# A hybrid decoder block on one core: new durations in the kernel's own scheduler, and one probability tile for two heads

## The chip, the cores and the metric

The kernel runs on one core of one Trainium2 chip. The metric is the device time of one execution in microseconds. The kernel does all its arithmetic in fp32: each large matrix product is made of three products of split operands (a high part times a high part, and two cross products of a high and a low part).

## The reference, cut to what matters

One decoder layer over 512 tokens of width 1024, then a final RMSNorm. The layer has one input projection whose columns feed three groups of heads, an output projection, and a feed-forward block of width 4096:

```
h = rmsnorm(x, norm1_w)
proj = h @ w_in
aq, ak, av, bq, bk, bv, br, ba, cq, ck, cv = split(proj)
y_a = dilated_attention(aq, ak, av, bias_a)          # 6 heads of 64
y_b = gla(bq, bk, bv, br, ba, w_a2, b_a, gla_norm_w)  # 4 heads, gated linear attention
y_c = moba_attention(cq, ck, cv, bias_c)              # 6 heads of 64
x = x + concat(y_a, y_b, y_c) @ w_out
x = x + square(relu(rmsnorm(x, norm2_w) @ w_ff1)) @ w_ff2
return rmsnorm(x, final_norm_w)
```

With 512 tokens the two kinds of softmax attention are plain causal attention with a bias that depends on the distance alone (a table of 640 values for each head), so the kernel treats the 12 heads of groups A and C alike, as six pairs.

## The kernel before, in words

**Stages.** The kernel first multiplies x with the columns for the gated linear attention (products `av`, `bq`, `bk`, until about 29 us), then makes queries and keys of the twelve softmax heads (`qkps`, two pieces of weights for each pair of heads, q and k), values and gates (`vps`), the gated linear attention (`lp`, `ktp`, `up`, `op`, `yp`), and for each pair of heads scores (`sps`), softmax, transposes (`ptp`) and values (`po`). Then come the output projection (`ops`), the norm and transposes (`yps`), and the feed-forward block in four slices of two layers (`f1X`, `f1Y`, `f1Z`, then `f2X`, `f2Y`, `f2Z`). The four large projections use a scheme of seven block products in place of eight, whose sums of weight blocks are made partly by accumulating DMA loads from POOL's queue.

**Weights.** Every piece of 128x1024 weights (`wraw`, 512 KB) is loaded, then cut: ScalarE rounds it to the high part `wh`, VectorE subtracts to make the low part `wl` (function `parts`). Activations are cut in the same way (`xh`/`xl`, `xsh`/`xsl`, `Ah`/`Al`).

**The start.** `scaled_x` makes `xh`, `xl` and the squares of x. `row_scale` sums the squares on TensorE (`rsp`) after six of the eight passes of the first product, and makes on VectorE `ss`, with ScalarE and VectorE `rstd`, then `diag` and the scale row `R`. `load_small` (L622) copies one column of x on POOL (tile `xT2`), so that what follows waits for that piece of x, and then issues ten loads of constants on POOL's queue: `cst`, `smask`, `hsel`, the bias table's inputs, `bav`, `wa2`, two pieces of `oneh`, `lmask` and `gw`.

**What sets the order.** No order is written out by hand. Each part of the work is a generator ("stream") that yields operations, waits for events, and takes and gives back counted resources (PSUM banks, weight buffers). The class `Plan` is a list scheduler that runs when the kernel is built: it keeps a clock for each engine, a time at which each tile is ready, and a clock each for the descriptor generator (`dge`) and for DMA. Among the operations at the heads of all streams it issues the one that can start first by its clocks, with the stream's priority to break ties. Issue order is queue order on the engine, so a wrong duration in the planner makes another order, not another duration. The durations stand in `Op.__init__` (`self.cost`, in microseconds):

- TensorE: an fp32 product with a contraction over 32 rows (the `lp` products of the gated linear attention, 112 of them) costs 0.031.
- VectorE: 0.075 + 1.04 ns an element, half the rate for copies and operations with scalars whose inputs are all in SBUF. There is no price of its own for the scan, for the masked copies (`copy_predicated`, which put the levels of the gated linear attention into `attn`), or for an operand that is one column read per partition.
- DMA: an ordinary load takes 0.47 on the `dge` clock, and its bytes at 320e3 per microsecond on the `dma` clock, whichever engine issues it, and is there 2.0 later.

Where an operation can run on either of two engines (`Any`), the planner takes the one that ends first. That is so for the scaling of probabilities by `rz` (VectorE or ScalarE) and for the copies of `th`, `q` and `k`.

Slots: most tiles of 128x512 or less share one tag of 52 buffers (`slot`). The planner does not count them; an operation that writes a slot still in use waits on the chip without the planner knowing. In `attention`, each head takes three slots for its probabilities: `P0` for query block 3, `P1` for blocks 2 and 0, and `P2`, half used, for block 1. `softmax` works on these in place: minimum and sum (`tensor_tensor_reduce`, written as `mn`), exponential on ScalarE with the sum `z`, reciprocal `rz`, and the scaling.

Of the kernel before, what the change touches and what calls it, by code (L numbers as in the profile page):

```python
# [9 lines left out]
F32 = mybir.dt.float32  # L10
# [26 lines left out]
class Op:  # L37


    def __init__(self, eng, method, args, kw):  # L40
        self.eng, self.method, self.args, self.kw = eng, method, args, kw
        self.out = args[0]
        outs = [args[0]]
        inner = [a for a in list(args[1:]) + [v for k, v in kw.items() if k != "accum_out"] if isinstance(a, bass.AP)]
        if kw.get("accum_out") is not None:
            outs.append(kw["accum_out"])
        if method == "tensor_tensor_reduce":
            outs.append(inner.pop())
        self.outs = [o.tensor.name for o in outs]
        self.ins = [a.tensor.name for a in inner] + (self.outs if "accum_op" in kw else [])  # L50
        n = 1
        for c in args[0].shape[1:]:
            n *= c
        self.mode = None
        if eng == "tensor":
            self.mode = inner[-1].shape[0] in (32, 64), args[0].shape[0] in (32, 64)
            wide, long = inner[-1].dtype == F32, max(n, 250) / 2400
            if method != "matmul":
                self.cost = 0.109
            elif wide and inner[-1].shape[0] == 32:  # L60
                self.cost = 0.031
            elif wide:
                self.cost = 0.002 + max(n / 600 / (1 + (args[0].shape[0] == 64)), 0.21)
            elif inner[-1].shape[0] == 64:
                self.cost = max(n / 2260, 0.12) / 2
            else:
                self.cost = 0.0135 + long
        elif eng == "scalar":
            few = sum(a.shape[-1] == 1 and n > 4 for a in inner) + ("accum_out" in kw)
            self.cost = 0.09 + n / 1200 + 0.093 * few  # L70
        elif eng == "vector":
            many = method in ("tensor_scalar", "tensor_copy") and all(a.space == bass.MemoryType.SB for a in inner)
            rate = 0.52 if many else 6.25 if method == "reciprocal" else 1.04
            if method == "tensor_reduce":
                n = 512
            self.cost = 0.075 + n * rate / 1000
        elif eng == "gpsimd":
            self.cost = 0.15 + n * (0.9 if method == "memset" else 2.1) / 1000
        if method == "dma_start":
            self.cost = 0.9 if "accum_op" in kw else 0.06  # L80
            self.rate = 170e3 if "accum_op" in kw else 320e3
            self.size = 4 * n * args[0].shape[0]
# [18 lines left out]
PE, ACT, DVE, POOL, SP = (Engine(n) for n in ("tensor", "scalar", "vector", "gpsimd", "sync"))  # L101


class Plan:
# [18 lines left out]
    def fire(self, key, t=None):  # L123
        self.done[key] = self.now if t is None else t
# [7 lines left out]
    def issue(self, op, at):  # L132
        getattr(getattr(self.nc, op.eng), op.method)(*op.args, **op.kw)  # L133
        t = self.start(op, at)
        end = t + op.cost
        if op.mode:
            end += SWITCH * (self.mode not in (None, op.mode))
            self.mode = op.mode
        self.clock[op.eng] = end
        if op.method == "dma_start":  # L140
            if "accum_op" in op.kw:
                self.clock["dma"] = max(self.clock["dma"], end + 1.0) + op.size / op.rate
                end = self.clock["dma"] + 3.0
            else:
                self.clock["dge"] = max(self.clock["dge"], t) + 0.47
                self.clock["dma"] = max(self.clock["dma"], self.clock["dge"] + 0.65) + op.size / op.rate
                end = self.clock["dma"] + 2.0
        for n in op.outs:
            self.ready[n] = max(self.ready.get(n, 0.0), end + self.LAT)
        return end  # L150
# [59 lines left out]
def hybrid_block_kernel(ctx: ExitStack, tc: tile.TileContext, xT_d, x_d, w0_d, wv_d, wqk_d, wo_d, w1_d, w2_d,  # L210
                        nw_d, ba_d, wa2_d, gw_d, fw_d, rb_d, oh_d, cst_d, lm_d, out_d):
    nc = tc.nc
    consts = ctx.enter_context(tc.tile_pool(name="consts", bufs=1))
# [10 lines left out]
    def slot(name, dt=F32, shape=(128, 512)):  # L224
        return sp.tile(list(shape), dt, name=name, tag="slot", bufs=SLOTS)
# [37 lines left out]
    alT = slot("alT", shape=(128, 512))  # L263
    xT = [slot("xT") for _ in range(KT)]
    tab = dr.tile([12, 640], F32, name="tab")
    xT2 = consts.tile([128, 1], F32)
    R, Rn8, ssx = slot("R"), slot("Rn8"), slot("ssx")
    xh = [slot("xh", F32R) for _ in range(KT)]
    xl = [slot("xl", F32R) for _ in range(KT)]
# [351 lines left out]

    def load_small():  # L622
        yield ("wait", ("xh", 1))
        yield POOL.tensor_copy(xT2, xT[2][:, :1])
        for t, d in ((cst, cst_d[:, 0:512]), (smask, cst_d[:, 512:1024]), (hsel, cst_d[:, 1024:1028]), (rb[:34, :12], rb_d),
                     (bav, ba_d), (wa2[:16], wa2_d)):
            yield POOL.dma_start(t, d)
        for i in range(2):
            yield POOL.dma_start(oneh[i][:34], oh_d[:, i * 320:(i + 1) * 320])
        fire("consts")  # L630
        spawn(bias_table(oneh), 1)
        yield POOL.dma_start(lmask, lm_d)
        yield POOL.dma_start(gw, bass.AP(tensor=gw_d.tensor, offset=gw_d.offset, ap=[[0, 128], [1, 256]]))
# [317 lines left out]
    def attention():  # L951

        yield ("wait", "tab")
        yield ("wait", "attn")
        for p in range(6):
            nb = []
            for e in range(2):
                nb.append(slot("nb"))
                yield SP.dma_start(nb[e], bass.AP(tensor=tab.tensor, offset=tab.offset + (2 * p + e) * 640, ap=[[1, 128], [1, 512]]))
            yield ("wait", ("qk", p))  # L960
            (qh, ql), (kh, kl) = st[p]
            P = []
            for e in range(2):
                A0, A1, A2 = slot("P0"), slot("P1"), slot("P2", shape=(128, 256))
                P.append([A1[:, 384:512], A2[:, 0:256], A1[:, 0:384], A0[:, 0:512]])
            for qbs in ((3, ), (2, 0, 1)) if p in (1, 2, 3, 4) else ((3,), (2, 0), (1,)):
                apart = len(qbs) > 1 and 1 in qbs
                sps, sps1 = [], []
                for e in range(2):
                    yield ("take", "s")  # L970
                    sps.append(bank("s", "sps"))
                    if apart:
                        yield ("take", "og"[e])
                        sps1.append(bank("og"[e], "sps"))
                ops, at, n0 = [], {}, 0
                for qb in qbs:
                    n = 128 * (qb + 1)
                    qs = slice(qb * 128, (qb + 1) * 128)
                    for e in range(2):
                        at[qb, e] = sps1[e][:, :n] if apart and qb == 1 else sps[e][:, n0:n0 + n]  # L980
                    for j, (qq, kk) in enumerate(((qh, kh), (ql, kh), (qh, kl))):
                        for e in range(2):
                            rows = slice(64 * e, 64 * e + 64)
                            ops.append(PE.matmul(at[qb, e], qq[rows, qs], kk[rows, :n], start=(j == 0), stop=(j == 2),
                                                 skip_group_check=True))
                    if not (apart and qb == 1):
                        n0 += n
                yield ops
                last = [x for x in qbs if not (apart and x == 1)][-1]
                for qb in qbs:  # L990
                    for e in range(2):
                        free = "og"[e] if apart and qb == 1 else "s" if qb == last else None
                        spawn(softmax(P[e][qb], at[qb, e], nb[e][:, 384 - 128 * qb:512], (p, e, qb), free), 1)
            give("big")
            give("big")
            if p == 5:
                give("w")
                fire("scores")
            for kbs in KBS:
                for e in range(2):  # L1000
                    spawn(turn(P[e], kbs, (p, e)), 0)

    turns = []

    def turn(P, kbs, key):
        for qb in range(min(kbs), NB):
# [6 lines left out]
        for kb in kbs:  # L1013
            off[kb] = n
            for qb in range(kb, NB):
                ops.append(PE.transpose(pt[:, n:n + 128], P[qb][:, kb * 128:(kb + 1) * 128], flip))
                n += 128
# [36 lines left out]

    def softmax(P, s, nb, key, last):
        mn, z, rz = (small(x, (128, 1)) for x in ("mn", "z", "rz"))
# [716 lines left out]
```

## Time and profile before

| | us |
|---|---|
| three runs | 564.97, 565.54, 566.04 |
| median | 565.54 |
| the profiled execution's own time | 565.34 |
| its span in the profile | 563.5 |

The span runs from the first to the last instruction that the profiler recorded; what lies around it is 1.84 us. The granted TensorE clock was 0.998 of full speed over the execution. In the rows that follow, a name such as `wl<-wraw,wh` says which tile an instruction writes and which it reads, `x138` how many such instructions there are, and a name after `<-` in an idle time says what ended it. PE is TensorE, PEld its weight loads, DVE VectorE, ACT ScalarE, POOL GpSimd and SP SyncE. All instructions carry the line of the planner's `issue` (L133), so groups are told apart by tile names.

### The profile page before, as it was taken

To read this page: it belongs to the slowest core of one execution; us is meant where nothing else is said; L and a number is where in the kernel's file an instruction comes from. 1 tells how busy PE (TensorE), PEld (TensorE's weight loads), DVE (VectorE), ACT (ScalarE), POOL (GpSimd) and SP (SyncE) were. 2 spreads that over 40 slices of the span, in tenths; PEclk is the share of its full clock that TensorE was granted. 3 is DMA by queue.
4 is the path that set the end of the run, shared out by engine and by line. 5 is a ranking of instruction groups with operands and counts; after the bars stand their busy time and mean duration, and the time that the engine had idled before them with its cause. 6 is when DMAs were issued, how large, how long until landed. Compare 5 with 4: busy or idle time off the path is not lost.

```text
span 563.5 us, 9460 instructions
## 1 busy us (share of the span) xinstructions
PE 554.7 (98%) x3513; PEld 478.4 (85%) x3513; DVE 480.4 (85%) x875; ACT 370.7 (66%) x658; POOL 69.7 (12%) x91
## 2 busy tenths in 40 slices
PE   9999999999999999999999999999999999999995
PEld 8978887867876768899987899988999888999884
DVE  7799999977868988999699995799957799867985
ACT  8664655884865775989766476855477654579553
POOL 5031110010000002110111010120020110011203
PEclk9999999999999999999999999999999999999999
DMA  8954685585124775992989429687378594395803
GB/s 317 393 123 123 128 217 124 161 335 103 38 43 127 242 150 115 271 272 60 274 212 204 163 64 278 201 151 204 113 158 283 121 201 158 95 220 113 150 12 137
DMA packets 29948, 96.58 MB, mean 171 GB/s; under 512 B 3648, under 2 KB 3690, under 8 KB 29904
## 3 DMA queue, kind: packets, MB, share of 16 engines
q0 software_dynamic: 9456, 33.53, 32.8%
q1 hardware_dynamic: 20160, 62.20, 31.5%
q8 instruction: 27, 0.44, 0.3%
q10 hardware_dynamic: 288, 0.27, 0.1%
q14 instruction: 17, 0.14, 0.1%
HBM read 93.86 MB, written 2.13 MB: 170 GB/s over the span
## 4 chain that ended last, share of the span: by engine, by line
PE 83%; DVE 11%; ACT 2%; issue 2%; DMA 2%; ACTq 0%; POOLq 0%
PE f2X L133 14%; PE f1X L133 13%; PE qkps L133 11%; PE f1Z L133 8%; PE ops L133 7%; PE f2Z L133 7%; PE f1Y L133 4%; PE vps L133 3%; PE f2Y L133 3%; DVE wl L133 3%; PE po L133 2%; PE ptp L133 2%; PE sps L133 2%; PE av L133 2%; DMA wraw<-in_w 2%
## 5 line engine op out<-in xcount | busy, mean ns | idle before, releaser
L133 DVE TENSOR_TENSOR wl<-wraw,wh 128x1024 fp32r<-128x1024 f32 (+2 forms) x174 | 192.0, 1111 | 38.2 <-ACT wh L133 37.2
L133 ACT ACTIVATE wh<-wraw 128x1024 fp32r<-128x1024 f32 (+2 forms) x173 | 164.7, 966 | 58.9 <-DMA wraw<-in_w 10.5
L133 PE MATMUL f1X<-yp,wh 128*128 128x256 f32 x512 | 92.7, 283 | 0.0
L133 PEld LDWEIGHTS f1X<-yp,wh 128*128 128x128 f32 x512 | 80.1, 192 | 0.3
L133 POOL DMA_DIRECT2D wraw<-in_w x46 | 40.8, 962 | 270.3 <-DVE wl L133 219.0
L133 PE MATMUL f1X<-yp,wl 128*128 128x256 f32 x256 | 72.5, 283 | 0.0
L133 PE MATMUL f2X<-wh,Al 128*128 128x512 f32 (+1 forms) x132 | 50.5, 383 | 0.0
L133 PE MATMUL f2X<-wh,Ah 128*128 128x512 f32 (+1 forms) x132 | 50.5, 383 | 0.0
L133 PE MATMUL f2X<-wl,Ah 128*128 128x512 f32 (+1 forms) x132 | 50.5, 383 | 0.0
L133 PEld LDWEIGHTS f1X<-yp,wl 128*128 128x128 f32 x256 | 49.1, 192 | 0.2 <-DVE wl L133 0.2
L133 PE MATMUL f1Z<-yp,wh 128*128 128x256 f32 x256 | 46.3, 283 | 0.0
L133 ACT ACTIVATE h<-h 128x512 f32<-128x512 f32 x56 | 34.7, 625 | 10.3 <-DVE h L133 9.8
L133 PE MATMUL qkps<-xh,wh 128*128 128x512 f32 x96 | 40.1, 417 | 0.0
L133 PEld LDWEIGHTS f1Z<-yp,wh 128*128 128x128 f32 x256 | 39.9, 192 | 0.0
L133 ACT ACTIVATE Ah<-h 128x512 fp32r<-128x512 f32 x40 | 24.0, 620 | 21.5 <-DVE h L133 21.5
L133 PE MATMUL qkps<-xh,wl 128*128 128x512 f32 x96 | 37.5, 391 | 0.0
L133 PE MATMUL qkps<-xl,wh 128*128 128x512 f32 x96 | 37.5, 390 | 0.0
L133 ACT ACTIVATE P<-P,mn 128x512 f32<-128x512 f32 (+3 forms) x48 | 26.6, 555 | 16.6 <-DVE mn L133 16.5
L133 PE MATMUL f1Z<-yp,wl 128*128 128x256 f32 x128 | 36.2, 283 | 0.0
L133 DVE TENSOR_TENSOR Al<-h,Ah 128x512 fp32r<-128x512 f32 x40 | 26.9, 687 | 3.2 <-ACT Ah L133 3.1
L133 PEld LDWEIGHTS f2X<-wl,Ah 128*128 128x128 f32 x132 | 24.8, 188 | 4.9
L133 PEld LDWEIGHTS f2X<-wh,Ah 128*128 128x128 f32 x132 | 24.8, 188 | 4.8
(266 smaller groups left out, 1223.9 us busy)
## 6 DMA issues: line engine op xcount, KB each, us to landing
wraw<-in_w SPq DMA_DIRECT2D x66, 512.0 KB, 5.2
wraw<-in_w POOLq DMA_DIRECT2D x46, 512.0 KB, 6.7
wraw<-in_wqk SPq DMA_DIRECT2D x12, 512.0 KB, 6.1
wraw<-in_wv SPq DMA_DIRECT2D x10, 512.0 KB, 8.6
wraw<-in_wv POOLq DMA_DIRECT2D x8, 512.0 KB, 6.0
wraw<-in_wo SPq DMA_DIRECT2D x8, 512.0 KB, 7.2
wraw<-in_wo POOLq DMA_DIRECT2D x8, 512.0 KB, 5.9
nb<-tab SPq DMA_DIRECT2D x12, 256.0 KB, 4.3
```

Of the source, the lines that this page charges most:

```text
L133: getattr(getattr(self.nc, op.eng), op.method)(*op.args, **op.kw)
```

## The change

The planner's prices are edited in five places, the two heads of a pair share the tile of block 1, and a tile is renamed:

- an fp32 product over 32 rows costs 0.0635 instead of 0.031;
- a scan costs 1.13; a masked copy 0.58 if the last dimension of its output is 1, else 0.33;
- any other VectorE operation with a one-column operand (and more than 4 elements), and every `scalar_tensor_tensor`, costs 0.055 more;
- an ordinary load from POOL's queue no longer advances the `dge` and `dma` clocks; it is there 3.0 plus its bytes at 80e3 per microsecond after its issue;
- `P2` becomes one tile of 128x2x256 for both heads, allocated once for each pair;
- the column that `load_small` copies is called `x2c`.

```diff
             elif wide and inner[-1].shape[0] == 32:
-                self.cost = 0.031
+                self.cost = 0.0635
...
             self.cost = 0.075 + n * rate / 1000
+            if method == "tensor_tensor_scan":
+                self.cost = 1.13
+            elif method == "copy_predicated":
+                self.cost = 0.58 if args[0].shape[-1] == 1 else 0.33
+            elif any(a.shape[-1] == 1 and n > 4 for a in inner) or method == "scalar_tensor_tensor":
+                self.cost += 0.055
...
             if "accum_op" in op.kw:
                 self.clock["dma"] = max(self.clock["dma"], end + 1.0) + op.size / op.rate
                 end = self.clock["dma"] + 3.0
+            elif op.eng == "gpsimd":
+                end += 3.0 + op.size / 80e3
             else:
                 self.clock["dge"] = max(self.clock["dge"], t) + 0.47
...
-    xT2 = consts.tile([128, 1], F32)
+    x2c = consts.tile([128, 1], F32)
...
-        yield POOL.tensor_copy(xT2, xT[2][:, :1])
+        yield POOL.tensor_copy(x2c, xT[2][:, :1])
...
             P = []
+            A2 = slot("P2", shape=(128, 2, 256))
             for e in range(2):
-                A0, A1, A2 = slot("P0"), slot("P1"), slot("P2", shape=(128, 256))
-                P.append([A1[:, 384:512], A2[:, 0:256], A1[:, 0:384], A0[:, 0:512]])
+                A0, A1 = slot("P0"), slot("P1")
+                P.append([A1[:, 384:512], A2[:, e], A1[:, 0:384], A0[:, 0:512]])
```

## The prediction, made before the changed kernel was run

> **What bounds the kernel now.** I read the page first, for the spread of work over the engines, then busy time by stage, then the waits of the weight loads, and last the order on VectorE and ScalarE where the stages looked thin.
>
> ```profile
> span 563.5 us, 9460 instructions
> PE 554.7 (98%) x3513; PEld 478.4 (85%) x3513; DVE 480.4 (85%) x875; ACT 370.7 (66%) x658; POOL 69.7 (12%) x91
> PE 83%; DVE 11%; ACT 2%; issue 2%; DMA 2%; ACTq 0%; POOLq 0%
> ```
>
> TensorE is busy 554.7 of 563.5 us and carries 83% of the chain that ended last. No product is added or removed by the change, so only the time in which TensorE does nothing can move. The table by stage says where that is (columns: busy us and count for each engine, granted clock, DMA share, GB/s).
>
> ```profile
> 0.00:24.00 24.00, 22.94 (x141) 21.21 (x141) 16.75 (x32) 17.40 (x30) 7.85 (x20) 1.00 0.95 346
> 24.00:47.00 23.00, 22.86 (x108) 18.00 (x108) 22.45 (x43) 13.50 (x20) 4.29 (x7) 1.00 0.66 190
> 76.00:92.00 16.00, 15.84 (x114) 12.48 (x111) 15.43 (x26) 9.69 (x13) 1.75 (x2) 1.00 0.69 162
> 92.00:106.00 14.00, 13.82 (x87) 11.22 (x85) 14.00 (x47) 7.10 (x18) 0.00 (x0) 1.00 0.32 84
> 106.00:122.00 16.00, 15.81 (x98) 12.04 (x100) 14.48 (x50) 15.52 (x38) 0.00 (x0) 1.00 1.00 366
> 264.00:300.00 36.00, 35.55 (x228) 32.16 (x228) 30.92 (x44) 25.81 (x42) 6.24 (x8) 1.00 0.94 228
> 300.00:555.00 255.00, 255.00 (x1605) 231.97 (x1604) 215.91 (x264) 158.77 (x219) 31.21 (x35) 1.00 0.64 160
> ```
>
> From 300 to 555 us there is nothing to win: 255.00 of 255 busy. Idle TensorE inside these stages is 0.14 + 0.16 + 0.18 + 0.19 + 0.45 = 1.12 us. That is too little, because a matmul's recorded length overlaps the next one's:
>
> ```profile
> 40.28 14.32 PE qkps L133 x63
> ```
>
> ```profile
> 38.63 0.39 PE L133 MATMUL qkps<-xh,wl 128*128 128x512 f32 x1
> 39.15 1.12 PE L133 MATMUL zps<-alT,misc 128*128 128x512 f32 x2
> ```
>
> In the chain 63 projection products take 14.32 us, 227 ns each, while the timeline records one as 0.39 us long; a pause shorter than the difference stays hidden.
>
> The waits of the weight loads between 28 and 125 us show those pauses (in total, times, longest):
>
> ```profile
> PEld sps L133 <- DVE mn L133: 1.0, 3, 0.4
> PEld ptp L133 <- ACT th L133: 0.6, 2, 0.4
> PEld zps L133 <- DVE alT L133: 0.6, 1, 0.6
> PEld ptp L133 <- ACT P L133: 0.6, 1, 0.6
> PEld vps L133 <- DVE v L133: 0.4, 1, 0.4
> PEld lp L133 <- DVE kq L133: 0.4, 1, 0.4
> PEld ptp L133 <- ACT v L133: 0.3, 1, 0.3
> ```
>
> These are 3.9 us, nearly all behind VectorE or behind ScalarE work that follows VectorE. In the same stages VectorE is full: 22.45 of 23 us, 15.43 of 16, 14.00 of 14. So from 24 to 122 us VectorE decides what little TensorE loses, and 3.9 + 0.45 (the stage 264 to 300) = 4.4 us is about the most that a better order could give, outside the head and the tail.
>
> **The change part by part.**
>
> *POOL's plain loads in the planner.* Before, each of load_small's ten loads (L622) adds 0.47 to the planner's descriptor clock and its bytes at 320e3 a microsecond to its DMA clock, ahead of SyncE's later loads. The queue's row for the first 24 us gives the bytes:
>
> ```profile
> q0 software_dynamic: 464, 0.98, 11.3%
> ```
>
> 0.98 MB put about 3.1 on the DMA clock, ten loads 4.7 on the other. After, they touch neither. I followed the two clocks and the three "raw" tokens by hand with the code's constants: the first wqk load lands at plan time 23 before and at about 19.5 after, the second at 25 before and 21 after. The row sums ss, which wait for the product rsp, stand near plan time 23.5 in both, since TensorE's first six passes set them. So before, the order is ss, then the low part wl of the first wqk piece; that is the order on the chip:
>
> ```profile
> 19.33 1.27 DVE L133 SCALAR_TENSOR_TENSOR xs<-xT,nw,xs 128x256 f32<-128x256 f32 x3
> 24.17 0.16 DVE L133 TENSOR_SCALAR ss<-rsp 128x4 f32<-128x4 f32 x1 [3.57 <-PE rsp L133]
> 24.25 1.23 DVE L133 TENSOR_TENSOR wl<-wraw,wh 128x1024 fp32r<-128x1024 f32 x1
> 19.32 1.04 ACT L133 ACTIVATE wh<-wraw 128x1024 fp32r<-128x1024 f32 x1
> 24.37 0.21 ACT L133 ACTIVATE rstd<-ss 128x4 f32<-128x4 f32 x1 [4.00 <-DVE ss L133]
> ```
>
> VectorE sat idle for 3.57 us in front of ss, ScalarE for 4.00 us in front of rstd, and both had work queued behind: wh of the first piece was done at 20.36. The second piece had landed too: its load is the one that the issue view shows between 10.3 and 10.6 us, with 10.6 us to landing, so at about 21.0.
>
> ```profile
> wraw<-in_wqk SPq DMA_DIRECT2D x1, 512.0 KB, 10.6
> ```
>
> After the change both wl stand ahead of ss in the order. The first runs from 20.4, the second from about 22.1 (its wh takes 1.04 from 21.0), ending at 23.3, before rsp lets ss go at 24.17. Two subtractions leave the full stretch; back to back they cost VectorE about 1.15 each (1.23 less the overlap with the next instruction), so it begins the stretch with 2.3 us less to do. ss itself is not delayed. What was late next in the stretch is visible: the product zps, above at 39.15, waited for alT:
>
> ```profile
> 38.43 0.67 DVE L133 COPY alT<-alps 16x512 f32<-16x512 f32 x1
> ```
>
> At 227 ns a product, after the one at 38.63, zps could have started at 38.86; it lost 0.3 us. I count that as gained.
>
> *The rest of the 3.9 us.* Without zps 3.3 us of named weight-load waits are left. The lead of 2.3 us on VectorE can take between nothing and all of them. VectorE waits for others on the way, for instance 0.68 us for lp in front of the copies at 76.57, and such a wait eats a lead. I take a third, 1.1 us, nearer to the lower end; both ends stay for the range.
>
> *Durations.* A scan takes 1.205 us as recorded and the plan had 0.61. A fused operation with a scalar column takes 746 ns where a plain one of the same shape takes 685, so 0.055 more is right. The masked copies run at 0.33 apart for the long levels, and the last ones at 0.65:
>
> ```profile
> L133 DVE TENSOR_TENSOR_SCAN b<-smask,la 128x512 f32<-128x512 f32 x1 | 1.2, 1205 | 0.0
> L133 DVE SCALAR_TENSOR_TENSOR xl<-xT,nw,xh 128x512 fp32r<-128x512 f32 x8 | 6.0, 746 | 0.0
> L133 DVE TENSOR_TENSOR tk<-qkps,R 128x512 f32<-128x512 f32 x6 | 4.1, 685 | 4.0 <-PE qkps L133 4.0
> 76.91 0.59 DVE attn L133 x2
> 77.90 1.31 DVE attn L133 x2
> 55.28 1.94 PE lp L133 x64
> ```
>
> The pair at 77.90 belongs to level 2, which the new rule (only a last dimension of 1) still prices at 0.33, so half of the slow copies stay mispriced. The narrow products: 64 records are 32 instructions, since each fp32 product is recorded twice, so 1.94/32 = 61 ns. The new 0.0635 is right, the old 0.031 was half. Over 112 such products the plan's TensorE ran 3.6 us ahead of itself. None of this changes the duration of an instruction on the chip; it changes which of two ready instructions is queued first. An operation queued one place too early costs about what one such wait shows, 0.3 to 0.4 us (sps, vps, ptp above). I allow three of them either way, so -1.2 to +1.2, and take 0, because the rows say which prices are better but not which neighbours swap.
>
> *Shared probability tile.* One slot in six is saved for each of six head pairs. Slots are what the bias loads nb wait for, on SyncE's queue, where the weight loads stand behind them:
>
> ```profile
> SPq L133 <- DVE s L133: 12.4, 1, 12.4
> SPq L133 <- PE op L133: 11.0, 1, 11.0
> ```
>
> TensorE did not pay for these waits: the rows of its waits name no DMA between 28 and 125 us. Shorter waits gain nothing and longer ones have that cover; a load late by more than it would show as a pause like those above, so -0.4 to +0.4, taken as 0. In the plan the two heads now also seem to wait for each other in block 1, a matter of order like the one before. The renamed column tile changes nothing.
>
> *Sum.* 565.34 (the profiled execution, 563.5 of span and 1.84 around it) - 0.3 - 1.1 = 563.94, said as 564.0. The median of the runs is 565.54, so the profiled one stands 0.20 below it, inside their spread of 564.97 to 566.04. This kernel can tell about 0.2%, 1.13 us, from no change: faster means below 564.41, slower above 566.67.
>
> **The rivals.** *The lead is lost.* The 2.3 us on VectorE are eaten by its own waits before 76 us and the new order behind it gains as often as it loses. For it speaks that TensorE is covered by other work nearly everywhere; against it, that VectorE is then full to 106 us. Only zps remains: 565.34 - 0.3 = 565.0, with 564.4 to 566.6 around it.
>
> *The first feed-forward block starves: slower.* The stage 264 to 300 is the one later place where TensorE has no other work. Its chain hangs on a transfer:
>
> ```profile
> 267.40 9.03 DMA wraw<-in_w
> 267.40 2.68 POOL L133 DMA_DIRECT2D wraw<-in_w  x3 [3.34 <-ACT wh L133]
> 298.55 0.95 ACT wh L133
> 299.51 5.71 PE f2Z L133 x24
> ```
>
> DMA is 0.94 busy there, the accumulating load took 9.03 us, and TensorE already lacks 0.45 us. The cuts that release this load are ordered by what attention leaves behind on VectorE and ScalarE. If the new order brings the release at 267.40 later by more than the slack that is left, about nothing, each microsecond costs one. One more step of the cut on each engine ahead of it (1.04 + 1.23) is 2.3 us: 565.34 - 0.3 + 2.3 = 567.3.
>
> *The planner now thinks loads too early.* If the loads really compete, pieces arrive after their planned place, and in-order engines block on them: VectorE in front of a wl with ss behind it. By what POOL's loads put on the DMA clock, 3.1 us later than planned: ss, and with it R and everything scaled, would move from 24.17 to 23.3 + 3.1 + 0.2 = 26.6, 2.4 us of VectorE time lost, and 565.34 + 2.4 = 567.7 if TensorE had no cover. It decides when the second wqk piece lands after about 21.9. The trace speaks against it: that piece landed at about 21.0 with these very loads in flight, near the new plan's 21, because the competition is in the trace already and the plan's tokens are late by themselves. [...]
>
> **How the numbers follow.** The forecast, 564.0, has 0.45, with 562.0 to 564.4 of its own: the lower end is 563.94 less half of the remaining 2.2 us and less most of the 1.2 of the order. The lost lead has 0.33. Starving has 0.17 and loads planned too early 0.05, so slower has 0.22. Faster 0.45, same 0.33, slower 0.22. A range that leaves out 2 in 10 reaches from 562.0 up through the lost lead into the starving case, 567.0.
>
> **What would show it.** Right: the wl of the first wqk piece and the next run between 20 and 24 us, the 3.57 us in front of ss shrink to about 1, zps comes before 38.9, and the weight loads' named waits up to 125 us shrink from 3.9 to about 2.5; after 300 us the stages are as long as before. Wrong in the first step: ss still ahead of wl. Wrong in the second: VectorE leads by 2 us at 47 us but the named waits stay at 3 us or more. Starved: TensorE's idle time from 264 to 300 us grows over 1 us with a wh or a transfer in front of it.

## The result, and the profile after

The changed kernel takes 569.37 us (median of 6 runs, 568.69 to 570.26); the kernel before, run beside it on the same chip, takes 565.72 (564.97 to 566.31). The ratio is 1.0066, with a 95% interval of 1.0056 to 1.0076: slower by 3.7 us, where 564.0 and a range of 562.0 to 567.0 had been forecast. The profiled execution took 569.06 us, with a span of 567.3 and a granted clock of 0.995 (0.998 before). In the changed kernel the planner's `issue` is L139. The ratios below leave out one slow execution, of the eleven of experiment 1's kernel: 683.42 us at a granted clock of 0.753.

The head of the page, and the table by stage with the columns of before (busy us and count of PE, PEld, DVE, ACT and POOL, granted clock, DMA share, GB/s):

```profile
span 567.3 us, 9459 instructions
PE 555.5 (98%) x3513; PEld 480.0 (85%) x3513; DVE 478.6 (84%) x868; ACT 373.3 (66%) x665; POOL 69.5 (12%) x91
```

```profile
0.00:24.00 24.00, 22.94 (x139) 21.29 (x140) 18.73 (x36) 19.44 (x34) 7.68 (x20) 1.00 0.96 347
24.00:47.00 23.00, 23.00 (x109) 18.40 (x108) 19.89 (x39) 11.02 (x18) 4.81 (x8) 1.00 0.65 189
106.00:122.00 16.00, 13.34 (x82) 11.60 (x81) 11.19 (x38) 10.52 (x26) 0.00 (x0) 0.89 0.76 279
264.00:300.00 36.00, 36.00 (x250) 33.72 (x250) 32.83 (x47) 28.08 (x46) 6.17 (x7) 1.00 0.94 226
300.00:555.00 255.00, 255.00 (x1601) 231.92 (x1600) 216.23 (x263) 158.96 (x217) 29.67 (x33) 1.00 0.64 158
```

Three rows tell the story. By 24 us VectorE has been busy for 1.98 us more than before (18.73 for 16.75): the lead that the prediction worked out is there at that point. From 24 to 47 us it is busy for 2.56 us less (19.89 for 22.45), but it also waits more, and at 47 us it is no longer ahead (the section on why the prediction was wrong shows the waits). From 106 to 122 us TensorE is busy for 13.34 of 16 us, 15.81 before, and the granted clock, 1.00 before, is 0.89. In the other stages TensorE's busy time agrees with before within half a microsecond, and the one from 264 to 300 has no idle time left.

What stands behind the bad row is in the chain of waits from 105 to 118 us (start, length, what):

```profile
104.94 1.41 PE sps L139 x16
106.35 4.19 PE op L139 x30
...
110.56 0.23 DVE sg L139
110.78 0.47 DVE P L139
...
113.38 0.60 DVE oB L139
...
114.02 0.97 PE ptp L139 x4
115.00 2.56 PE vps L139 x6
117.56 0.76 PE ptp L139 x6
118.31 1.40 PE vps L139 x6
```

Before, `op`, the last products of the gated linear attention, ran from 98.9 to 104 us, ahead of the second head pair's scores (the `sps` at 103.91 are the first pair's last); three rows of before's timeline:

```profile
98.89 1.11 PE L133 MATMUL op<-vB,attn 128*128 128x64 f32 x8
102.97 1.00 PE L133 MATMUL op<-vB,attn 128*128 128x64 f32 x8
103.91 0.62 PE L133 MATMUL sps<-k,q 64*128 64x256 f32 x6
```

Now that pair's scores stand in front of it, six products from 101.4 us and the 16 that the chain counts right before it, and it ends at 111.4. Behind it the chain leaves TensorE: the next step is VectorE's `sg`, then seven steps on the probabilities `P`, and `oB`, and only then the transposes `ptp`. These can't start before `oB`: `op` fills both PSUM banks that the transposes use (tag `pt` in the kernel), and `oB` reads the banks out. Note also the two groups of six `vps` products: the first takes 2.56 us, the second 1.40.

The timeline of VectorE and TensorE over that place (start, length, engine, operation, idle time before it and what ended it) shows the two pauses:

```profile
105.98 0.16 DVE L139 RECIPROCAL rz<-z 128x1 f32<-128x1 f32 x1
110.56 0.23 DVE L139 TENSOR_SCALAR sg<-v 128x128 f32<-128x128 f32 x1 [4.42 <-PE op L139]
```

```profile
114.02 0.97 PE L139 MATMUL ptp<-cst,P 128*128 128x128 f32 x4 [2.67 <-DVE oB L139]
```

`sg` reads only `v`, and the last `v` written before it was done at 105.7 (104.97 + 0.75 in the timeline); no data ties it to `op`. What ties it is the buffer. The 52 buffers of the shared tag are handed out in turn, and by the order of allocation the tile `sg` gets the buffer that `eq` had, an operand of `op`. The second pair's `P1` tiles follow with the buffers of `s2m` and `attn`, and the third pair's bias loads with those of `vB` and `m`, all read by `op`. VectorE stands for 4.42 us at `sg`, with the second pair's probabilities and `oB` queued behind, and starts none of them meanwhile. TensorE, whose queue has `ptp` behind `op`, sits idle for 2.67 us as recorded (the wait of its weight load is 2.8, which the expectations below use).

The same place in narrow windows, with the columns of the table above (the granted clock is the third number from the right):

```profile
111.00:114.00 3.00, 0.36 (x4) 0.22 (x2) 3.00 (x17) 3.00 (x11) 0.00 (x0) 1.00 0.92 317
114.00:116.00 2.00, 1.98 (x7) 1.77 (x8) 2.00 (x11) 2.00 (x7) 0.00 (x0) 0.55 1.03 414
116.00:118.00 2.00, 2.00 (x9) 1.53 (x8) 2.00 (x5) 1.55 (x3) 0.00 (x0) 0.59 1.03 422
```

The windows' mean clocks, 0.55 and 0.59, make 2 x 2 x 0.45 + 2 x 2 x 0.41 = 3.4 us at half the clock right behind the pause. That is the slow group of `vps`: 2.56 / 6 = 427 ns a product, 1.40 / 6 = 233 in the next.

### The profile page after: what moved, and what is told of

Same layout as the page of the kernel before. It is cut to its first block, busy times and chain, and to the rows that moved or that the text cites. A ratio compares the mean times of both kernels' runs of the same rounds, so it can differ in the third digit from the quotient of the medians.

```text
span 567.3 us, 9459 instructions
## 1 busy us (share of the span) xinstructions
PE 555.5 (98%) x3513; PEld 480.0 (85%) x3513; DVE 478.6 (84%) x868; ACT 373.3 (66%) x665; POOL 69.5 (12%) x91
## 4 chain that ended last, share of the span: by engine, by line
PE 92%; DVE 4%; ACT 2%; issue 1%; ACTq 0%; DVEq 0%
PE f1X L139 16%; PE f2X L139 15%; PE qkps L139 12%; PE f2Z L139 8%; PE f1Z L139 7%; PE ops L139 6%; PE vps L139 6%; PE f1Y L139 4%; PE f2Y L139 4%; PE ptp L139 2%; PE sps L139 2%; PE av L139 2%; PE po L139 2%; PE bk L139 1%; PE bq L139 1%; PE lp L139 1%
## 5 line engine op out<-in xcount | busy, mean ns | idle before, releaser
L139 DVE TENSOR_TENSOR wl<-wraw,wh 128x1024 fp32r<-128x1024 f32 (+2 forms) x174 | 192.0, 1111 | 39.9 <-ACT wh L139 39.3
L139 ACT ACTIVATE wh<-wraw 128x1024 fp32r<-128x1024 f32 (+2 forms) x173 | 164.8, 966 | 53.4 <-PE f2X L139 14.2
L139 PE MATMUL f1X<-yp,wh 128*128 128x256 f32 x512 | 92.8, 283 | 0.1
L139 PEld LDWEIGHTS f1X<-yp,wh 128*128 128x128 f32 x512 | 80.2, 192 | 0.6 <-DVE yp L139 0.3
L139 POOL DMA_DIRECT2D wraw<-in_w x46 | 40.8, 984 | 270.2 <-DVE wl L139 244.9
L139 PE MATMUL f1X<-yp,wl 128*128 128x256 f32 x256 | 72.4, 283 | 0.0
L139 PE MATMUL f2X<-wh,Al 128*128 128x512 f32 (+1 forms) x132 | 50.5, 383 | 0.0
L139 PE MATMUL f2X<-wh,Ah 128*128 128x512 f32 (+1 forms) x132 | 50.5, 383 | 0.0
L139 PE MATMUL f2X<-wl,Ah 128*128 128x512 f32 (+1 forms) x132 | 50.5, 383 | 0.0
L139 PEld LDWEIGHTS f1X<-yp,wl 128*128 128x128 f32 x256 | 49.1, 192 | 0.0
L139 PE MATMUL f1Z<-yp,wh 128*128 128x256 f32 x256 | 46.6, 284 | 0.2 <-DVE yp L139 0.2
L139 ACT ACTIVATE h<-h 128x512 f32<-128x512 f32 x56 | 34.7, 625 | 9.4 <-DVE h L139 9.0
L139 PEld LDWEIGHTS f1Z<-yp,wh 128*128 128x128 f32 x256 | 40.0, 192 | 0.5 <-DVE yp L139 0.4
L139 PE MATMUL qkps<-xh,wh 128*128 128x512 f32 x96 | 40.2, 419 | 0.0
L139 PE MATMUL qkps<-xh,wl 128*128 128x512 f32 x96 | 37.5, 391 | 0.0
L139 PE MATMUL qkps<-xl,wh 128*128 128x512 f32 x96 | 37.5, 390 | 0.0
L139 ACT ACTIVATE Ah<-h 128x512 fp32r<-128x512 f32 x40 | 24.3, 621 | 19.4 <-DVE h L139 19.2
L139 PE MATMUL f1Z<-yp,wl 128*128 128x256 f32 x128 | 36.2, 283 | 0.0
L139 ACT ACTIVATE P<-P,mn 128x512 f32<-128x512 f32 (+3 forms) x48 | 26.5, 554 | 14.2 <-DVE mn L139 14.0
L139 DVE TENSOR_TENSOR Al<-h,Ah 128x512 fp32r<-128x512 f32 x40 | 26.8, 686 | 3.2 <-ACT Ah L139 3.2
L139 PEld LDWEIGHTS f2X<-wl,Ah 128*128 128x128 f32 x132 | 24.8, 188 | 4.9
L139 PEld LDWEIGHTS f2X<-wh,Al 128*128 128x128 f32 x132 | 24.8, 188 | 4.8
```

## The experiments

All were timed in five rounds against the kernel before on the same chip. Theory: **slots**, as above: the new order lets the second pair run ahead of `op`, its tiles use up the buffers that only `op` gives back, and VectorE blocks. Rivals: **POOL price** (loads now planned too early), **shared tile** (the two heads of a pair wait for each other), and, for the size, **clock** (how much of the loss is the half clock).

**1. Only `op`'s place put back.** The second pair's attention may not begin before `op` is issued; all new prices and the shared tile stay.

```diff
         yield ops
+        fire("op")
...
         for p in range(6):
+            if p == 1:
+                yield ("wait", "op")
             nb = []
```

> The changed kernel, with the attention of the second pair of heads held back in the planner until the product op of the gated linear attention is issued. Slot theory (op is queued behind the second pair's scores, the slots run out, and what is written next waits for op): the pause of 2.7 us behind op and the 25 us wait of the bias load on SyncE go, and the time comes back to 565 to 566.5. Rival, POOL's loads priced too early: nothing in that is touched, 569. Rival, the shared tile ties the two heads together: untouched, 569.

Measured: 566.23 beside 565.72, ratio 1.0007 (0.9997 to 1.0016). The chain and the stage's row of this kernel:

```profile
105.76 4.81 PE op L139 x38
110.58 0.44 PE ptp L139 x4
111.02 0.89 PE sps L139 x6
```

```profile
106.00:122.00 16.00, 16.00 (x104) 13.42 (x104) 13.14 (x35) 12.15 (x23) 0.00 (x0) 1.00 0.76 272
```

`op` is as late as in the changed kernel (105.76 for 106.35), yet `ptp` follows it at once and the clock stays at 1.00: VectorE is not blocked (5.88 us busy from 106 to 114, where the changed kernel has 0.57 + 3.00 = 3.57), and the first half of `oB` runs at 108.0 us, while `op` is still going. This one wait takes back 3.1 of the 3.7 us, with the changes of order behind it counted in. The kernel keeps POOL's new price and the early start on VectorE (19.91 us busy from 24 to 47, as in the changed kernel), and is no faster than before: the early start gains nothing.

**2. Level 2 priced right.** The slow price for masked copies goes to a last dimension of 2 as well.

```diff
-                self.cost = 0.58 if args[0].shape[-1] == 1 else 0.33
+                self.cost = 0.58 if args[0].shape[-1] <= 2 else 0.33
```

> The changed kernel, with the masked copies of level 2 priced at 0.58 like those of level 1. The planner then issues op before the second pair's scores again. Slot theory: 564.5 to 566.5, no pause behind op. Rivals (loads priced too early; shared tile): both parts are still in, 569.

Measured: 567.39, ratio 1.0029 (1.0018 to 1.0040), a little above what was expected. The pause behind `op` is gone (16.00 busy of 16 from 106 to 122); in its place stand small ones between 195 and 220 us (0.98 the longest). A second change of order without the block, and again without the loss at this place.

**3. One part at a time, on the kernel before.** First the price of POOL's loads alone, then the shared tile alone.

```diff
+            elif op.eng == "gpsimd":
+                end += 3.0 + op.size / 80e3
```

> The kernel before, with the new price of POOL's loads alone. The order that comes out has op behind the second pair's scores and the slots run out there. Slot theory: 568 to 570, with a pause behind op. Loads priced too early: also 568 to 570, but with the loss before 50 us, at waits for weights. Shared tile: 565.7, since the tile is not shared.

Measured: 571.71, ratio 1.0108 (1.0087 to 1.0129). `op` is late here too, and the pause with it; windows of this kernel:

```profile
114.00:116.00 2.00, 1.94 (x7) 1.58 (x7) 2.00 (x7) 2.00 (x9) 0.00 (x0) 0.50 1.02 416
116.00:118.00 2.00, 1.53 (x7) 1.11 (x6) 2.00 (x8) 1.83 (x3) 0.00 (x0) 0.50 1.04 418
118.00:122.00 4.00, 4.00 (x18) 3.27 (x17) 3.43 (x4) 2.67 (x5) 0.00 (x0) 0.69 0.65 248
```

The half clock lasts twice as long, 6.5 us in these rows. The price alone does this damage, but by the same place and not by loads that come too late: experiments 1 and 2 carry the price and are free of it. TensorE also stands for 1.34 us at 34 us in this kernel, behind ScalarE's `vB`, which is no load.

```diff
+            A2 = slot("P2", shape=(128, 2, 256))
             for e in range(2):
-                A0, A1, A2 = slot("P0"), slot("P1"), slot("P2", shape=(128, 256))
-                P.append([A1[:, 384:512], A2[:, 0:256], A1[:, 0:384], A0[:, 0:512]])
+                A0, A1 = slot("P0"), slot("P1")
+                P.append([A1[:, 384:512], A2[:, e], A1[:, 0:384], A0[:, 0:512]])
```

> The kernel before, with the shared probability tile alone. Op stays early. Slot theory and loads priced too early: 565 to 566.5, the same as before. Shared tile: 568 to 570.

Measured: 567.29, ratio 1.0023 (1.0015 to 1.0032): a miss by 0.8 us. The shared tile by itself costs 1.3 us. Its `op` is early and it has no pause of that kind; the loss is spread in small pieces that I can't name.

**4. One buffer more, one less.** The changed kernel with 53 slots (smaller pools elsewhere make the room) and with 51.

```diff
-BIGS, SLOTS, WPAIRS = 25, 52, 5
+BIGS, SLOTS, WPAIRS = 25, 53, 5
```

> The changed kernel with 53 slots instead of 52 (the memory comes from unused copies of small tiles; the planner does not count slots, so its order stays). Slot theory: what is written after op moves on by one slot; the gate tile then follows a tile that op reads a little earlier, so VectorE's wait ends earlier by something between 0.3 and 2 us: 567 to 569, under the changed kernel. Rivals (loads priced too early, shared tile, or op late by itself): 569.4, no change.

> The changed kernel with 51 slots. Slot theory: transposes of pair 0 now wait for op as well, the pause behind op grows by 0.5 to 3 us: 570 to 573. Rivals: 569.4.

Measured: 569.31 with 53 (ratio 1.0057, 1.0045 to 1.0070), just above what was expected, and 570.98 with 51 (1.0092, 1.0078 to 1.0106). The traces tell more than the times. With 53, VectorE's timeline (`op` runs from 106.84 us there):

```profile
109.73 0.23 DVE L139 TENSOR_SCALAR sg<-v 128x128 f32<-128x128 f32 x1 [3.10 <-PE op L139]
111.06 0.56 DVE L139 CUSTOM_DVE_ANT_0 P<-sps,nb 128x384 f32<-128x384 f32 x1 [1.10 <-PE op L139]
```

With 51, the chain:

```profile
106.44 2.38 PE op L139 x18
108.82 0.02 issue
108.84 0.61 ACT th L139
109.45 0.04 issue
109.49 2.04 PE op L139 x12
```

One buffer more, and `sg` gets one that `op` gives back sooner: its wait falls from 4.42 to 3.10 us. But the next tile in turn, a `P`, then waits for `op` for another 1.10 us, so VectorE comes free no earlier. One less, and a second engine is caught: ScalarE's `th` waits in the middle of `op`, and `op` in turn for ScalarE. That the places and lengths of the waits move with the number of buffers, while the order of work stays, shows that buffers are what is waited for. One more is far too few to help.

**5. TensorE's price alone.** The kernel before with 0.0635 for the narrow products.

> The kernel before, with the new price of the narrow fp32 products alone. In the order that comes out op is again behind the second pair's scores and the slots run out. Slot theory: 567.5 to 570, with a pause behind op and a long wait of a bias load on SyncE. Loads priced too early, shared tile: neither is in, 565.7.

Measured: 575.14, ratio 1.0160 (1.0146 to 1.0175). The sign was right, the size far off. `op` is late, with pauses of 2.08 and 1.33 us behind it and a half clock of 6.8 us; and a second stretch at half clock, which nothing had announced, begins at 63.9 us.

**6. Is it lateness or buffers?** The kernel before with the shared tile, and `op` held back by hand until the second pair's first scores are issued.

```diff
+        yield ("wait", ("scored", 1, 3))
         yield ops
...
                 yield ops
+                fire(("scored", p, qbs[0]))
```

> The kernel before with the shared tile, and op forced in the planner behind the first scores of the second pair; no price is changed. The slots do not run out here: the shortest distance between a slot's last use and its next is 15 instructions near op. If the slots are what costs, 566 to 567.5 (the shared tile alone took 567.3). If it costs merely that op is late, 568 to 570.

Measured: 567.27, ratio 1.0024 (1.0015 to 1.0034), the same as the shared tile without it (567.29).

```profile
103.85 0.90 PE sps L133 x6
104.75 5.01 PE op L133 x38
109.76 0.23 PE ptp L133 x2
```

`op` stands behind scores and runs six microseconds later than before, for nothing. So here lateness costs nothing: `op` fills the same two banks, and nothing that TensorE needs waits for one of the 52 buffers.

**7. Is it VectorE or the load queue?** In the changed kernel SyncE's queue waits for `op` too, with the third pair's bias loads (25.4 us) and weight loads behind them. Here these loads go to POOL's queue; the order on TensorE, VectorE and ScalarE is the same.

```diff
-                yield SP.dma_start(nb[e], ...)
+                yield (POOL if p == 2 else SP).dma_start(nb[e], ...)
```

> The changed kernel with the two bias loads of the third pair issued from POOL's queue instead of SyncE's; the order on TensorE, VectorE and ScalarE is the same. It tells apart which of the two blocks behind op costs time. If it is the 25 us on SyncE, with five pieces of query and key weights behind it: those land 15 us or more earlier and the time is 565.5 to 567.5. If it is VectorE, which waits in order for a slot that op reads: 569 to 570, no change, and the pause behind op stays at 2.7 us.

Measured: 569.79, ratio 1.0072 (1.0060 to 1.0084), as slow as the change, with the same 2.67 us in front of `ptp`. SyncE's long wait costs nothing. The half clock is there too, 0.70 as a mean from 114 to 118 us, though the loads have moved and the DMA share is 0.20 in that window.

**8. The change less one price.** Without POOL's price, and without TensorE's.

> The changed kernel without the new price of POOL's loads; the prices of TensorE and VectorE and the shared tile stay. In this order op stands late, but the slots that are written right after it had their last use 10 instructions earlier or more. Slot theory: 566 to 568, a pause behind op of at most 1 us. Loads priced too early: 565 to 566. If any late op costs 4 us: 569 to 570.

> The changed kernel without the new price of the narrow products; POOL's price, VectorE's prices and the shared tile stay. Op comes before the second pair's scores. Slot theory: 565 to 567.5, no pause behind op. Loads priced too early: 569, since that price is in.

Measured: 570.27 without POOL's price (ratio 1.0084, 1.0071 to 1.0097), a miss by 2.3 us, and 566.83 without TensorE's (1.0017, 1.0008 to 1.0025). Without TensorE's price `op` is early and there is no pause. Without POOL's there is none behind `op` either, though `op` starts at 111.9 us, later than in the changed kernel (the second sign that lateness alone is free); but there is another one, in front of `vps` at 68 us:

```profile
66.00:68.00 2.00, 0.10 (x1) 0.00 (x0) 0.99 (x2) 1.92 (x7) 0.00 (x0) 1.00 0.95 320
68.00:70.00 2.00, 1.83 (x19) 1.31 (x21) 2.00 (x7) 0.75 (x3) 0.86 (x1) 0.71 0.00 0
```

TensorE waits 2.07 us for ScalarE's `dg` and goes on at half clock (0.50 from 70 to 74 us). That ScalarE's queue was itself behind is read from the chain; no run took it away.

**9. VectorE's prices and the shared tile, on the kernel before.**

> The kernel before with VectorE's prices and the shared tile alone. Op comes early. Slot theory: 565 to 567.5. It is also the candidate for a version that is not slower than before: if VectorE's prices are worth something by themselves, it is under the 567.3 of the shared tile alone.

Measured: 570.42, ratio 1.0084 (1.0070 to 1.0098), a miss by 2.9 us. `op` stands ahead of the second pair's scores and nothing pauses behind it. The trace, of the longest of the five executions (571.88 us), has pauses of 1.27 us (`vps`, at 68), 1.03, 0.77 and 1.61 us (transposes and scores between 194 and 204) and 3.4 us at half clock behind the last. No run takes these away one by one, and the half clock is not in all executions: two, of 569.80 and 570.42 us, had a granted clock of 0.998 in place of 0.994. So each of the three groups of corrected prices (VectorE's together with the shared tile) brings, by itself, an order slower than the old one, and not always at the same place.

**10. How much of the loss is the clock?** Spare products behind `op`, read by nobody, keep TensorE busy in the pause; every other instruction keeps its place.

```diff
         yield ops
+        idle = bank("o", "idle")
+        for _ in range(11):
+            nc.tensor.matmul(idle, xh[0][:, :128], xh[1], start=True, stop=True)
```

> The changed kernel with 11 spare products of 128x512 (xh times xh, into an unused bank, read by nobody) queued on TensorE directly behind op; no other instruction changes its place on any engine. At the 0.23 us that such a product takes in the chain they fill 2.5 of the 2.8 us pause. Theory, that the pause halves TensorE's clock and that this half clock costs about 1.7 us on top of the pause: ptp starts at 114.0 as before, the granted clock stays 1.00 from 114 to 118, vps products come every 0.23 us, and the time falls from 569.4 to about 567.7 (567.2 to 568.3). Rival, that something else halves the clock (the burst of loads at 109 to 120 us, or the products themselves): clock 0.55 as before and 569.4. Second rival, that the half clock is hidden behind VectorE anyway: clock 1.00 and still 569.0 or more.

> The changed kernel with 5 spare products of 128x512 behind op in place of 11: they fill 1.1 us and leave a pause of about 1.7 us. If the clock is halved only by a pause of over 2 us, the result is that of eleven products, about 567.7 and clock 1.00; if 1.7 us is long enough, the clock is 0.55 again and the time 569.4.

Measured: 569.20 with eleven (ratio 1.0063, 1.0049 to 1.0077), 568.56 with five (1.0053, 1.0040 to 1.0066). Their bank came free late, so both began at 113.1 to 113.2 us and filled only the end of the pause. With eleven:

```profile
113.07 2.80 PE L872 MATMUL idle<-xh 128*128 128x512 f32 x11 [1.20 <-DVE mn L139]
```

With five, and two windows behind them:

```profile
113.20 1.40 PE L872 MATMUL idle<-xh 128*128 128x512 f32 x5 [1.20 <-DVE mn L139]
114.66 0.65 PE L139 MATMUL ptp<-cst,P 128*128 128x128 f32 x4
...
116.97 0.99 PE L139 MATMUL ptp<-cst,P 128*128 128x128 f32 x6 [0.26 <-ACT th L139]
```

```profile
114.00:116.00 2.00, 1.94 (x11) 1.39 (x10) 2.00 (x12) 2.00 (x8) 0.00 (x0) 1.00 1.01 399
116.00:118.00 2.00, 1.74 (x11) 1.11 (x10) 2.00 (x6) 1.56 (x5) 0.00 (x0) 1.00 1.04 424
```

A recorded pause of 1.20 us in place of 2.67 leaves the clock at 1.00 in both: the pause is what halves it, not the loads, which are the same (DMA share 1.01 to 1.04). With five, `ptp` starts 7.67 us after `op` as in the changed kernel (114.66 - 106.99; 114.02 - 106.35), and the third group of `vps` ends 14.67 us after `op`'s start (121.66 - 106.99) in place of 15.41 (121.76 - 106.35). So the full clock gains 0.74 us there, and 0.81 in the medians (569.37 - 568.56; the two intervals overlap). The expected gain of 1.7 us was too high: at full clock TensorE meets the next wait, for ScalarE's `th` (0.26 us above), and less than half remains. With eleven, `ptp` comes 1.34 us later after `op` (9.01 us, 115.87 - 106.86) and the third `vps` group still ends 0.48 us sooner (14.93, 121.79 - 106.86): by itself the half clock costs 1.8 us, and what is left of it depends on the next wait.

**The account.** 569.37 - 565.72 = 3.65 us. Of these 3.14 hang on the place of `op` (569.37 - 566.23, experiment 1): about 0.8 by the half clock (experiment 10), the other 2.3, by subtraction, by the pause and the order behind it. The remaining 0.5 lies within what experiment 1's interval leaves open.

## Why the prediction was wrong, step by step

*What bounds the kernel.* TensorE's lost time moved, as said, and its clock with it, which the prediction did not have. The 4.4 us that a better order could give at most is a bound on gains; nothing in it limits what a new order can lose, and the prediction had no such bound.

*POOL's loads in the planner.* Half right, up to 24 us. One `wl` went ahead of `ss` in place of two, and VectorE's idle time in front of it fell from 3.57 to 1.40 us, ScalarE's in front of `rstd` from 4.00 to 0.35:

```profile
20.02 1.22 DVE L139 TENSOR_TENSOR wl<-wraw,wh 128x1024 fp32r<-128x1024 f32 x1
23.43 0.16 DVE L139 TENSOR_SCALAR ss<-rsp 128x4 f32<-128x4 f32 x1 [1.40 <-PE rsp L139]
23.50 1.22 DVE L139 TENSOR_TENSOR wl<-wraw,wh 128x1024 fp32r<-128x1024 f32 x1
23.62 0.21 ACT L139 ACTIVATE rstd<-ss 128x4 f32<-128x4 f32 x1 [0.35 <-DVE ss L139]
```

VectorE's lead, forecast as 2.3 us, was 1.98 at 24 us. It did not last: from 24 to 47 us VectorE stands idle for 0.4 + 0.5 + 0.5 + 1.7 = 3.1 us (before `Rn`, `tq`, `alT` and `la`), and that is why it is busy for 2.56 us less there. The longest of these waits hangs on `zps`:

```profile
41.13 1.02 PE L139 MATMUL zps<-alT,misc 128*128 128x512 f32 x2
42.91 0.75 DVE L139 TENSOR_SCALAR la<-zps,bav 128x512 f32<-128x512 f32 x1 [1.67 <-ACT ab L139]
```

The wait of `zps` is gone from the list of weight-load waits, but `zps` itself comes two microseconds later than before (39.15), not before 38.9, and the scan `b`, which follows from it, at 47.82 in place of 46.69. So the step "it begins the stretch with 2.3 us less to do" held, and the gain drawn from it did not.

*The rest of the 3.9 us.* Wrong. A third of 3.3 us was to go; experiment 1, which has the same start and no block, stands at 1.0007. Its weight loads no longer wait for `mn` and `zps`, but its narrow products `lp` have a new pause of 0.43 us at 66 us, behind ScalarE's `attn`, and there are three more of 0.25 to 0.37 us between 199 and 217.

*Shared probability tile, and durations.* This is the step that failed. The prediction read from SyncE's waits that slots run short, and priced a slot wait at -0.4 to +0.4 because "TensorE did not pay for these waits". It looked at the loads only. The same 52 buffers serve VectorE's and ScalarE's outputs, an engine that waits for one holds all that is queued behind it (4.42 us at `sg`), and which instruction waits is set by the order. The price measured 3.1 us, its half clock included. The bound for a change of order, three places at 0.3 to 0.4 us, was taken from the waits of an order without such a block; the runs with one part alone lost from 1.3 us (the shared tile, 0.0023 x 565.7) to 9.1 us (TensorE's price, 0.0160 x 565.7), so -1.2 to +1.2 was too narrow by far on the upper side.

*The rivals.* The lead was lost, as the first rival had it, in the change and in experiment 1; it accounts for the gain that did not come, not for the loss. The feed-forward block did not starve: 36.00 busy of 36 us. Loads planned too early: the price alone is slower by 1.08%, but the pause is the one behind the late `op`, as with TensorE's price, which has nothing to do with loads; experiments 1, 2 and the second kernel of 8 carry POOL's price and lose 0.4, 1.6 and 1.0 us. The mechanism that decided had no rival of its own.

*What stays open.* Where the shared tile alone loses its 1.3 us; whether ScalarE's late `dg` (experiments 8 and 9) is the whole cause of those pauses; and why no run with corrected prices came out ahead of the old order (the best, experiment 1, is no different from it), beyond the lead that was used up by 47 us. The planner doesn't count slots, which is the reason at one place, not shown for the others.

## What to carry to other kernels

A planner's better durations are only worth something if it also models what makes the engines wait: here one unmodelled buffer pool cost 3.1 us, and the corrected prices brought nothing that shows. When an edit can change the order of work, look for resources that are handed out in turn, ask which tile's last reader comes late in the new order, and what stands behind the waiting instruction on its engine. And price the risk of an order from one with such a block, not from the small waits of a tuned one.

## What the runs showed of the hardware

In these runs TensorE's clock was halved behind recorded pauses of two microseconds and more. Pauses of 2.07 (experiment 8), 2.08 (5), 2.43 (3), 2.53 and 2.79 (4) and 2.67 us (the changed kernel and experiment 7) each brought 3.4 or 6.8 us at half clock, worked out from the windows' granted clocks as above, with 128x512 products 427 ns apart in the changed kernel in place of 227 (the kernel before) to 233; pauses of 1.20 (experiment 10, twice), 1.27 (9) and 1.34 us (3) did not. One of 1.61 did, with others close before it, in the traced execution of experiment 9. The two executions of that kernel at a granted clock of 0.998 have room for 2 x 0.0025 x 568 = 2.8 us at half clock at most, so it did not happen there each time. With TensorE's price alone (experiment 5) a half clock began at 63.9 us with no recorded pause of over 0.46 us between 58 and 64, amid the 64 records of narrow `lp` products, and it lasted with next to no loads (DMA share, the second number from the right, 0.04 and 0.00; windows with the columns above):

```profile
63.00:66.00 3.00, 3.00 (x62) 2.88 (x60) 2.04 (x7) 1.58 (x4) 0.00 (x0) 0.65 0.04 7
66.00:69.00 3.00, 3.00 (x8) 2.32 (x9) 2.32 (x6) 1.11 (x2) 0.00 (x0) 0.50 0.00 0
```

What brought it there, no run shows.
